# A hybrid decoder block in float32 pairs: norm statistics from rows of x, and an opening that runs two whole GLU tiles on unnormalised x

## The chip, the cores and the metric

The kernel runs on one core of a Trainium2 chip. The metric is the time of the whole program in device microseconds, the median of three runs. The engines are TensorE (PE, matmuls), VectorE (DVE), ScalarE (ACT), GpSimd (POOL) and SyncE (SP), which issues all the transfers here.

## The reference, cut to what matters

One decoder layer over 2048 positions of width 1024. An RMS norm is followed by one wide projection into GLU halves, a convolution gate, queries, keys, values, an attention gate and merge gates. A depthwise convolution branch (31 taps, layer norm, SiLU) and a windowed attention branch are gated, projected, merged and projected again, with a residual and a final RMS norm.

```
def rmsnorm(x, g):
    y = x * lax.rsqrt(jnp.mean(x * x, axis=-1, keepdims=True) + RMS_EPS)
    return y * g

h = rmsnorm(x, norm_g)
proj = h @ w_in      # glu a, glu b, conv gate, q, k, v, attention gate, merge gates
c = silu(layernorm(depthwise_conv(a * sigmoid(b)), ln_g, ln_b))
y_conv = (c * silu(conv_gate)) @ w_conv_out
y_attn = (attention(rope(q), rope(k), v) * silu(attn_gate)) @ w_attn_out
x = x + (g_conv * y_conv + g_attn * y_attn) @ w_out
return rmsnorm(x, final_norm_g)
```

The statistic of the norm is one number per position: the mean of 1024 squares. A projection of normalised x is the projection of `x * g` times that position's `1 / rms`.

## The kernel before, in words

The positions are taken in two sweeps (`NSWEEP`) of 1024, and each sweep in two halves of `TH` = 512. Within a sweep x is held transposed: eight tiles `k` of 128 channels by 512 positions per half. Each float32 operand is split into a rounded part `hi` and the rest `lo` (`split_lo`, L233), and one `product` (L269) is three matmuls of 128x128 by 128x512. An output tile of 128 channels takes eight products per half. In the rows, `whi` and `wlo` are the parts of a weight, `hT` those of the normalised x, `u` those of `x * g` without the norm. `mm_` and a name is the PSUM tile of an item: `gb` and `ga` for the GLU, `ka`, `kb`, `q_a`, `q_b`, `v`, then the gates, `ya`, `yc`, and `o` for the last projection.

TensorE's instructions run in the order in which the program writes them. The other engines' orders and SP's queue are chosen at compile time by a list scheduler, by priority and readiness; program order gives the priority, and `tc.high_priority` raises it. At run time every engine takes its instructions in order.

`Line` (L159) is a planner with a clock of its own. It runs items, each a prefetch and a generator of blocks. The prefetch of an item is called ahead of the blocks of the item before it. Each block yields its cost on TensorE (`MM_US` = 0.2275 a matmul). In `spend` (L167) the clock moves on, background operations (`bg`) are taken one per `every` microseconds, and chains that are due are advanced. The convolution is background work: 31 operations on VectorE per channel tile, queued when a GLU tile's second half has left PSUM (`ev_a`, L532), one per 3.2 us (`ROPE_EVERY`) until attention starts and one per 2.4 us (`CONV_EVERY`) from then. When the last of eight tiles is done, `ln_chain` (L801) and `ln_chain2` (L813) put four matmuls each for mean and variance into TensorE's order, and then `ln_recip`, `ln_apply` and `u_op` (L839) follow as background operations, one per 1.6 us. `u_op` loads a stored gate (`lcg`), multiplies and splits. The first `ya` item's eviction (L901) writes `mp`, whose slot the last reader of the convolution's result must have freed; if the first `u_op`s have not been issued by then, it calls `line.finish()`, which issues all the rest ahead of it.

`norm_chain` (L324) takes the sum of squares per position, still spread over 128 partitions, splits it, multiplies it with `ones` (1/1024 in every cell), which sums over partitions and puts the mean into all of them, and takes the root and the reciprocal of 128x512 numbers into `rs`.

`opening` (L354) is the start of sweep 0. `first_blocks` runs `gb`, `ga` and `ka` of half 0 on `u` as the x tiles land, with the squares on ScalarE and their sums on VectorE beside it. Then `kb`, `q_a` and `q_b` of half 0 run on `u`, while the squares of half 1 are summed on POOL; the norm of half 1 stands after three products of the last of them. `both_halves_done` runs `gb` and `ga` of half 1 on `hT`, and the four remaining items run their half 1 on `hT`, while `put_h` (L344) makes the tiles of half 0. What was computed on `u` is multiplied by `rs` when it leaves PSUM (`un`, L396). From then on all items read `hT`. A second GLU tile follows at index 6 of `others`, by `GLU_AFTER`.

In the last projection of sweep 0, `prepare` (L965) gets sweep 1's x ready after each output block: `next_square` loads column tiles (`xs`), squares them on ScalarE and sums on POOL, `next_norm` starts the chain after blocks 4 and 8 (its matmuls come 6 us later on the planner's clock), and `next_h` loads again (`xh`) and makes `hT`.

Of the kernel before, what the change touches and what calls it, by code (L numbers as in the profile page):

```python
# [12 lines left out]
F32 = mybir.dt.float32  # L13
# [40 lines left out]
def hybrid_block(ctx: ExitStack, tc: tile.TileContext, x, xt, par_d, w_in, w_conv, sinks, w_attn, w_out,  # L54
# [181 lines left out]
    def load_w(src, name, home=None, steps=None):  # L236
# [4 lines left out]
        def part(kh):  # L241
# [74 lines left out]
    def add_square(raw, total, k, name, eng):  # L316
        if k == 0:
            act.activation(out=total, in_=raw, func=AF.Square)
        else:
            sq = t2k(name)  # L320
            act.activation(out=sq, in_=raw, func=AF.Square)
            eng.tensor_tensor(out=total, in0=total, in1=sq, op=ALU.add)

    def norm_chain(total, rs, wait, name):  # L324

        hi, lo = (t2k(f"{name}{p}", F32R) for p in "hl")
        act.copy(hi, total)
        split_lo(lo, total, hi, dve)
        yield 0.0, wait
        ms = small_bank(f"{name}ms")  # L330
        for i, part in enumerate((hi, lo)):
            pe.matmul(out=ms, lhsT=ones, rhs=part, start=(i == 0), stop=(i == 1))
        act.activation(out=rs, in_=ms, func=AF.Sqrt, bias=eps)
        for i in range(2):
            c = rs[:, i * (TH // 2):(i + 1) * (TH // 2)]
            dve.reciprocal(out=c, in_=c)
# [17 lines left out]
    def opening(items, load_rope):  # L354


        (pa, pb, pc_), rest = [it[2] for it in items[:3]], [it[2] for it in items[3:]]
        xr = [slot(A[i], [P, 2, TH], F32, f"xr0_{i}") for i in range(4)]
        raw = [[xr[k // 2][:, k % 2] for k in range(KC)], []]
        u = [slot((C[0:7] + A[5:6])[k], [P, 2, TH], F32R, f"u{k}") for k in range(KC)]  # L360
        total = work.tile([P, 2, TH], F32, tag="ln0", name="total0", bufs=1)
        rs = slot(X[0], [P, 2, TH], F32, "rs0")
        homes = [[slot(H[3 * i + j], [P, 2, 4, P], F32R if j else F32, f"w{i}_{j}") for j in range(3)]
                 for i in range(2)]
        ws, steps = [], []
        for i, (src, name, _) in enumerate((pa, pb)):
            steps.append([])
            ws.append(load_w(src, name, homes[i], steps[i]))
        steps.append([])
        ws.append(load_w(pc_[0], f"{pc_[1]}0", None, steps[2]))  # L370
        stats = {}

        def ready(k):
            load_x(0, 0, k, raw[0][k])
# [726 lines left out]
```

## Time and profile before

| What | us |
|---|---|
| median of three runs | 2057.91 (2057.75 to 2058.42) |
| the profiled execution's own time | 2059.32 |
| span of the profile | 2057.4 |
| mean granted TensorE clock | 0.988 of full |

The profile's page gives the busy time of each engine, then the span in 40 slices, the queues, the chain that ended last and the costliest groups of instructions. A group's row has the line, the engine, the operation, the tiles written and read, their shapes, and the count; behind the first bar stand the busy time in us and the mean of one in ns, behind the second the idle time of the engine ahead of it and what ended that. A timeline row has the start and the length in us, then engine, line, operation and tiles. A row of the waits has who waited, for whom, the total in us, how often, and the longest.

### The profile page before, as it was taken

How to read it: one execution, taken by the hardware profiler on the slowest of the kernel's cores; microseconds unless marked ns; L12 is line 12 of the kernel's file. 1: busy time of each engine (PE TensorE's matmuls, PEld its weight loads, DVE VectorE, ACT ScalarE, POOL GpSimd, SP SyncE). 2: the span in 40 equal slices, each digit the busy share in tenths (PEclk: the TensorE clock that was granted, in tenths of full speed). 3: DMA queues.
4: the chain of work that ended last, by engine and by line, in shares of the span. 5: the costliest groups of instructions: out<-in, count | busy, mean ns of one | idle time of the engine just before them, and what ended most of it. 6: DMA issues, size and time to landing. Idle time of an engine off the chain costs nothing.

```text
span 2057.4 us, 27299 instructions
## 1 busy us (share of the span) xinstructions
PE 2001.0 (97%) x9136; PEld 1660.0 (81%) x9136; DVE 1356.2 (66%) x1921; ACT 1025.7 (50%) x2249; POOL 439.1 (21%) x354
## 2 busy tenths in 40 slices
PE   6899999999999996999999999999999999999998
PEld 4688888888888884888788888888888888888887
DVE  7889679989995156123559686699888935341324
ACT  5432377767777354112432324777777774621222
POOL 5234332333233222243301020110111010000200
PEclk9899999999999998999999999999999999999999
DMA  7445555455556755446455356555555568474432
GB/s 253 148 135 174 174 180 164 159 178 179 164 176 206 249 190 193 149 139 231 160 184 165 110 165 215 165 177 170 171 166 167 179 222 261 165 242 148 148 118 82
DMA packets 269852, 361.14 MB, mean 176 GB/s; under 512 B 28560, under 2 KB 126992, under 8 KB 269712
## 3 DMA queue, kind: packets, MB, share of 16 engines
q1 hardware_dynamic: 269712, 359.40, 53.7%
q8 instruction: 72, 1.18, 0.2%
q14 instruction: 68, 0.56, 0.1%
HBM read 239.75 MB, written 119.54 MB: 175 GB/s over the span
## 4 chain that ended last, share of the span: by engine, by line
PE 59%; DVE 1%; DMA 1%; issue 0%; ACT 0%; DVEq 0%; SPq 0%; ACTq 0%
PE mm_yc L271 8%; PE mm_ya L271 8%; PE o L1025 7%; PE mm_ma L271 4%; PE mm_cg L271 4%; PE mm_ag L271 4%; PE mm_gb L271 4%; PE mm_ga L271 4%; PE mm_mc L271 4%; PE mm_q_b L271 2%; PE mm_q_a L271 2%; PE sc L683 1%; PE ov L733 1%; PE mm_v L271 1%; PE tpp L713 1%; PE mm_ka L271 1%
## 5 line engine op out<-in xcount | busy, mean ns | idle before, releaser
L507 DVE SCALAR_TENSOR_TENSOR acc<-glu,par,acc 128x1024 f32<-128x1024 f32 x464 | 596.1, 1285 | 6.2
L271 PE MATMUL mm_ya<-aT,whi_ya 128*128 128x512 f32 x512 | 159.4, 393 | 20.3 <-DVE mp L906 20.3
L1025 PE MATMUL o<-wo,mT 128*128 128x512 f32 x768 | 175.1, 389 | 1.0 <-DVE wo L234 1.0
L1025 PEld LDWEIGHTS o<-wo,mT 128*128 128x128 f32 x768 | 144.1, 188 | 31.3 <-DVE wo L234 1.4
L271 PE MATMUL mm_ma<-hT,whi_ma 128*128 128x512 f32 x512 | 159.7, 393 | 0.0
L271 PE MATMUL mm_cg<-hT,whi_cg 128*128 128x512 f32 x512 | 159.7, 393 | 0.0
L271 PE MATMUL mm_ag<-hT,whi_ag 128*128 128x512 f32 x512 | 159.4, 393 | 0.0
L271 PE MATMUL mm_mc<-hT,whi_mc 128*128 128x512 f32 x512 | 158.0, 390 | 0.0
L271 PE MATMUL mm_yc<-uT,whi_yc 128*128 128x512 f32 x512 | 157.6, 389 | 0.0
L724 POOL TENSOR_SCALAR_AFFINE_SELECT pc<-pt 128x1024 fp32r<-128x1024 f32 x60 | 65.6, 1094 | 422.5 <-DVE pt L234 416.7
L271 PE MATMUL mm_gb<-hT,whi_gb 128*128 128x512 f32 x480 | 149.5, 393 | 0.0
L271 PE MATMUL mm_ga<-hT,whi_ga 128*128 128x512 f32 x480 | 149.1, 392 | 0.0
L271 PEld LDWEIGHTS mm_ya<-aT,whi_ya 128*128 128x128 f32 x512 | 97.1, 190 | 41.0 <-DVE mp L906 20.7
L271 PEld LDWEIGHTS mm_yc<-uT,whi_yc 128*128 128x128 f32 x512 | 96.1, 188 | 19.9
L271 PEld LDWEIGHTS mm_mc<-hT,whi_mc 128*128 128x128 f32 x512 | 96.0, 188 | 20.1
L271 PEld LDWEIGHTS mm_ag<-hT,whi_ag 128*128 128x128 f32 x512 | 94.2, 188 | 18.3
L271 PEld LDWEIGHTS mm_cg<-hT,whi_cg 128*128 128x128 f32 x512 | 94.1, 188 | 18.3
L271 PEld LDWEIGHTS mm_ma<-hT,whi_ma 128*128 128x128 f32 x512 | 94.1, 188 | 18.2
L703 ACT ACTIVATE ss<-ss,st 128x128 f32<-128x128 f32 x256 | 99.7, 391 | 11.2 <-DVE st L698 10.6
L271 PEld LDWEIGHTS mm_ga<-hT,whi_ga 128*128 128x128 f32 x480 | 88.8, 188 | 17.6
L271 PEld LDWEIGHTS mm_gb<-hT,whi_gb 128*128 128x128 f32 x480 | 88.5, 188 | 17.5
L271 PE MATMUL mm_ya<-aT,wlo_ya 128*128 128x512 f32 x256 | 100.3, 392 | 0.0
(436 smaller groups left out, 4319.2 us busy)
## 6 DMA issues: line engine op xcount, KB each, us to landing
qk<-d_q SPq DMA_DIRECT2D x256, 64.0 KB, 2.2
d_a<-ss SPq DMA_DIRECT2D x128, 128.0 KB, 1.9
aT<-d_a SPq DMA_DIRECT2D x32, 512.0 KB, 5.5
qk<-d_k SPq DMA_DIRECT2D x240, 64.0 KB, 2.0
raw_ag<-in_w_in_dram SPq DMA_DIRECT2D x32, 256.0 KB, 3.8
d_ag<-ag SPq DMA_DIRECT2D x32, 256.0 KB, 2.2
ss<-d_ag SPq DMA_DIRECT2D x64, 128.0 KB, 2.6
raw_cg<-in_w_in_dram SPq DMA_DIRECT2D x32, 256.0 KB, 3.4
```

The lines of the kernel that those rows point to most:

```text
L271: pe.matmul(out=ps, lhsT=a, rhs=b, start=(k == 0 and i == 0), stop=(k == KC - 1 and i == 2))
L507: dve.scalar_tensor_tensor(out=to, in0=glu[c][:, j:j + T], scalar=tap(c, j), in1=acc[c], op0=ALU.mult, op1=ALU.add)
L683: pe.matmul(out=o, lhsT=q[:, h, :], rhs=r, start=(j == 0), stop=(j == 1))
L703: act.activation(out=sb[:, h, :], in_=sb[:, h, :], func=AF.Exp, scale=SCALE, bias=ngm[:, h:h + 1], accum_out=den[:, h:h + 1])
L713: pe.transpose(out=tpp[:, h, :], in_=sb[:, h, :], identity=ident)
L724: pool.affine_select(out=pc, in_=f(pt), pattern=[[0, 2], [0, GQ], [1, P]], compare_op=ALU.is_ge, fill=0.0, base=0, channel_multiplier=-1)
L733: pe.matmul(out=ov, lhsT=vv, rhs=pp[:, i % 2], start=(i == 0), stop=(i == nm - 1))
L1025: pe.matmul(out=ps, lhsT=a[:, c0:c0 + P], rhs=r, start=(k == 0 and i == 0), stop=(k == KC - 1 and i == 2))
```

## The change

Five things change.

1. The sum of squares comes from rows. A tile of 128 positions by 1024 channels of x is loaded, and one ScalarE instruction squares it and sums along the row (`row_square`), which gives one number per partition; four such tiles make a half. The root and the reciprocal are taken of 128x4 numbers. A diagonal matrix of 128x512 with these numbers (`dg`) is split, and the matmul with `ones` spreads each number to all partitions; a copy scaled by 1024 writes `rs`. The wide root and reciprocals and the sums on VectorE and POOL are gone.
2. The opening runs both halves of two GLU tiles (four items) on `u` and no key or query item. It loads, in this order: x of half 0 with the first two weights between, x of half 1, two row tiles of half 0, the third and the fourth row tile of half 0, each followed by one of the other two weights, the four row tiles of half 1, the sinks. The norm of half 0 stands in TensorE's order after 35 products, that of half 1 after 51 of the 64.
3. `hT` of half 0 is made after the fourth item's first half and `hT` of half 1 after the third item's second half; the first reader of either is `ka`, behind the opening.
4. In both sweeps the two value items come ahead of the query items, and the second GLU tile is no longer at index 6.
5. For sweep 1, `next_square` loads half rows (128 positions by 512 channels) instead of column tiles, and `next_norm` starts after blocks 3 and 7.

Also, in the opening both weight steps of an item are split on VectorE instead of the first one only.

```diff
-                split_lo(lo, raw, hi, dve if steps is not None and kh == 0 else pool)
+                split_lo(lo, raw, hi, dve if steps is not None else pool)
...
-    def add_square(raw, total, k, name, eng):
-        if k == 0:
-            act.activation(out=total, in_=raw, func=AF.Square)
-        else:
-            sq = t2k(name)
-            act.activation(out=sq, in_=raw, func=AF.Square)
-            eng.tensor_tensor(out=total, in0=total, in1=sq, op=ALU.add)
+    def row_square(x, out_, ss):
+        act.activation(out=out_, in_=x, func=AF.Square, accum_out=ss)
+
+    def norm_chain(ss, bank, rs, wait, name):
+        rt = work.tile([P, 2, 4], F32, tag="rt", name=f"{name}rt")
+        act.activation(out=rt[:, 0], in_=ss, func=AF.Sqrt, bias=eps, scale=1.0 / D)
+        dve.reciprocal(out=rt[:, 1], in_=rt[:, 0])
+        dg = t2k(f"{name}d").rearrange("p (b t) -> p b t", t=P)
+        dve.tensor_tensor(out=dg, in0=ident.unsqueeze(1).broadcast_to([P, 4, P]),
+                          in1=rt[:, 1].unsqueeze(2).broadcast_to([P, 4, P]), op=ALU.mult)
+        dg = dg.rearrange("p b t -> p (b t)")
         hi, lo = (t2k(f"{name}{p}", F32R) for p in "hl")
-        act.copy(hi, total)
-        split_lo(lo, total, hi, dve)
+        act.copy(hi, dg)
+        split_lo(lo, dg, hi, dve)
         yield 0.0, wait
-        ms = small_bank(f"{name}ms")
+        ms = bank()
         for i, part in enumerate((hi, lo)):
             pe.matmul(out=ms, lhsT=ones, rhs=part, start=(i == 0), stop=(i == 1))
-        act.activation(out=rs, in_=ms, func=AF.Sqrt, bias=eps)
-        for i in range(2):
-            c = rs[:, i * (TH // 2):(i + 1) * (TH // 2)]
-            dve.reciprocal(out=c, in_=c)
+        act.activation(out=rs, in_=ms, func=AF.Copy, scale=float(D))
...
+        def prefetch2():
+            for k in range(KC):
+                load_x(0, 1, k, raw[1][k])
+            for half in range(2):
+                for j in range(4):
+                    r0 = (4 * half + j) * P
+                    nc.sync.dma_start(out=rows[half][j], in_=x2[r0:r0 + P, :])
+                    if half == 0 and j > 1:
+                        for kh in range(2):
+                            steps[j][kh]()
+            load_sinks()
...
+            for half in range(2):
...
+                for k in range(KC):
+                    scaled_split(u[half][k], raw[half][k], k)
+                    for i in range(2):
+                        product(ps[i, half], ws[i][0](k), u[half][k], k)
                         yield 3 * MM_US
+            squares(0)
...
+                    if i == 2 and k == 2:
+                        yield spread(half)
+                        if half == 0:
+                            squares(1)
...
+                if half == 0 and i == 3:
+                    ht[0] = make_tiles(h_tags[0], 0, "hT0_")
+                    for k in range(KC):
+                        put_h(ht[0][k], raw[0][k], rs[:, 0], k)
+                if half == 1 and i == 2:
+                    ht[1] = make_tiles(h_tags[0], 1, "hT0_")
+                    for k in range(KC):
+                        put_h(ht[1][k], raw[1][k], rs[:, 1], k)
...
+        yield prefetch, first_blocks
+        yield prefetch2, later(2, 0)
+        yield (lambda: None), later(3, 0)
+        yield (lambda: None), later(2, 1)
+        yield (lambda: None), later(3, 1)
...
-        others = rope_items("k", E_K, store_k)
+        others = rope_items("k", E_K, store_k) + [v_item(i) for i in range(2)]
...
-            yield from opening(glu_items(0) + others[:4], load_rope)
-            glu_after.pop(0)
+            yield from opening(glu_items(0) + glu_items(1))
+            glu_after = glu_after[2:]
...
+        def next_square(b):
+            if b % 4 == 0:
+                nx["ss"] = work.tile([P, 3, 4], F32, tag="ss", name=f"ss{s + 1}_{b}")
+            r0 = (s + 1) * T + b * P
+            for i in range(2):
+                raw = raw_tile(f"xs{s + 1}_{b}_{i}")
+                nc.sync.dma_start(out=raw, in_=x2[r0:r0 + P, i * TH:(i + 1) * TH])
+                row_square(raw, t2k(f"sq{s + 1}_{b}_{i}"), nx["ss"][:, i, b % 4:b % 4 + 1])
...
-            if i in (4, 8):
-                line.start(next_norm(i // 4 - 1))
+            if i in (3, 7):
+                line.start(next_norm(i // 4))
```

`spread(half)` runs `norm_chain` at high priority and then `leave` for the first two items: multiply by `rs`, then the item's own eviction. `later(i, half)` runs one half of the third or fourth item.

More of the change, by code (lines that the diff above doesn't have):

```diff
@@ L352, in hybrid_block, with opening @@
     ht = [None, None]
[L354 to L361, printed above, removed]
+    def opening(items):
+        parts = [it[2] for it in items]
+        names = [A[0:4], A[14:16] + X[1:3]]
+        raw = []
+        for half in range(2):
+            pair = [slot(t, [P, 2, TH], F32, f"xr{half}_{t}") for t in names[half]]
+            raw.append([pair[k // 2][:, k % 2] for k in range(KC)])
+        u = [[slot(t, [P, 2, TH], F32R, f"u{half}_{t}") for t in tags]
+             for half, tags in enumerate((C[0:6] + A[4:6], A[6:11] + A[13:14] + H[14:16]))]
+        rows = [[slot(t, [P, D], F32, f"row_{t}") for t in tags]
+                for tags in (H[8:12], H[12:14] + H[6:8])]
@@ L362, in opening @@
         rs = slot(X[0], [P, 2, TH], F32, "rs0")
[L363 to L364 removed]
+        ss = work.tile([P, 2, 4], F32, tag="ss0", name="ss0", bufs=1)
+        acc = cv_ps.tile([P, T], F32, tag="acc", name="rs_bc")
         ws, steps = [], []
[L366 removed]
+        for i, (src, name, _) in enumerate(parts):
+            home = [slot(H[3 * i + j], [P, 2, 4, P], F32R if j else F32, f"w{i}_{j}")
+                    for j in range(3)] if i < 2 else None
@@ new lines, in leave, with squares @@
+        def leave(i, half, ps):
+            with tc.high_priority(offset=PRIO):
+                t = t2k(f"un{i}_{half}")
+                dve.tensor_tensor(out=t, in0=ps, in1=rs[:, half], op=ALU.mult)
+                parts[i][2](half, t)
+        ps = {}
+        def squares(half):
+            for j in range(4):
+                row_square(rows[half][j], rows[half][j], ss[:, half, j:j + 1])
+        def first_blocks():
+            for half in range(2):
+                for i in range(2):
+                    name = f"mm_{parts[i][1]}0{half}"
+                    ps[i, half] = (small_bank(name) if half and i else
+                                   mm_ps.tile([P, TH], F32, tag="mm", name=name))
+                for k in range(KC):
+                    scaled_split(u[half][k], raw[half][k], k)
+                    for i in range(2):
+                        product(ps[i, half], ws[i][0](k), u[half][k], k)
@@ L408, in first_blocks, with spread @@
                         yield 3 * MM_US
-            for k in range(2):
-                ws[2][1](k)
+            squares(0)
+        def spread(half):
+            chain = norm_chain(ss[:, half], lambda: acc[:, half * TH:(half + 1) * TH], rs[:, half], 0.0, f"n{half}")
             with tc.high_priority(offset=2 * PRIO):
-                steps_ = list(norm_chain(total[:, 0], rs[:, 0], 0.0, "n0"))
-            yield sum(us for us, _ in steps_)
-            with tc.high_priority(offset=PRIO):
-                for p, b in zip((pa, pb, pc_), ps):
-                    after_rs(p[2])(0, b)
@@ L463, in opening @@
-        yield (lambda: None), both_halves_done
-        def put_some(ks):
-            if ks[0] == 0:
-                ht[0] = make_tiles(h_tags[0], 0, "hT0_")
-            for k in ks:
-                put_h(ht[0][k], raw[0][k], rs[:, 0], k)
-        for i, (src, name, evac) in enumerate([pc_] + rest):
-            pre, blocks, _ = project(src, lambda k, half: ht[1][k], f"{name}1", evac, (1,))
-            def with_h(blocks=blocks, i=i):
-                put_some((2 * i, 2 * i + 1))
-                yield from blocks()
-            yield pre, with_h
+                us = sum(c[0] for c in chain)
```

118 lines of the change are left out of this document (35 added, 83 removed).

## The prediction

> **What bounds the kernel now.** I read the page's engine table first, then the list of what TensorE waited for, then the busy time by stretches of the span, then single rows of the timeline around the two places that these views point to.
>
> ```profile
> span 2057.4 us, 27299 instructions
> ...
> PE 2001.0 (97%) x9136; PEld 1660.0 (81%) x9136; DVE 1356.2 (66%) x1921; ACT 1025.7 (50%) x2249; POOL 439.1 (21%) x354
> ```
>
> TensorE is busy for 97% of the span, so the change can win only what TensorE loses in gaps and at a low clock, unless it alters the matmuls. It doesn't: the opening has 96 `product` calls of three matmuls and four matmuls with `ones` for the same outputs, before and after.
>
> ```profile
> PE mm_ya L271 <- DVE mp L906: 20.3, 1, 20.3
> PE n1ms L332 <- ACT n1h L327: 12.9, 1, 12.9
> PE mm_gb L271 <- ACT w L249: 7.9, 1, 7.9
> PE mm_gb L271 <- ACT hT L340: 4.2, 2, 2.8
> PE mm_gb L271 <- DVE hT L341: 1.9, 2, 1.6
> ```
>
> Columns: total, times, longest. Nearly all idle time stands here. Four of the five rows lie in the opening. The first is at the seam of sweep 0, where the first `ya` tile cannot leave PSUM.
>
> ```profile
> 0.00:14.40 14.40, 6.51 (x18) 4.44 (x19) 8.37 (x18) 9.80 (x17) 2.06 (x9) 1.00 0.84 293
> 14.40:40.40 26.00, 26.00 (x115) 21.20 (x113) 22.45 (x21) 15.01 (x26) 17.17 (x12) 1.00 0.78 259
> 40.40:53.30 12.90, 0.02 (x1) 0.00 (x0) 10.84 (x11) 3.42 (x7) 10.12 (x7) 0.62 0.61 214
> 62.20:75.00 12.80, 9.46 (x22) 6.43 (x23) 12.52 (x18) 5.14 (x8) 3.90 (x3) 0.60 0.45 144
> 787.00:807.00 20.00, 0.00 (x0) 0.00 (x0) 12.84 (x22) 6.53 (x11) 5.71 (x2) 0.60 0.54 186
> ...
> 102.81 0.39 PE L271 MATMUL mm_v<-hT,whi_v 128*128 128x512 f32 x1
> ...
> 1067.65 10.88 PE mm_ga L271 x48
> ```
>
> A stretch lists PE, PEld, DVE, ACT and POOL busy (with counts), then the granted clock, DMA share and GB/s. The last row is from the chain: 48 matmuls in 10.88 us, 0.2267 each at full clock, 0.68 a product. The opening's 292 matmuls are worth 66.2 us and `mm_v`, the first item behind them, starts at 102.81: the opening loses 36.6 us. Of that 10.3 fall before 14.4 (18 matmuls, 4.1 us of work), 12.9 in the wait for `n1h`, 6.1 in the waits for `hT`, and the other 7.3 are half clock: 0.60 granted from 62.2 to 75.
>
> **The start.** Squares and sums leave ScalarE's and VectorE's queues; the two first weights' splits go wholly to VectorE. A `k` has now two products, 1.36 us, against one x tile and half a weight step on ScalarE (0.72 + 0.3) and VectorE (0.74 + 0.35), by these rows:
>
> ```profile
> L340 ACT ACTIVATE hT<-xr,par 128x512 fp32r<-128x512 f32 x8 | 5.5, 718 | 4.8 <-PE mm_gb L271 4.6 <-DVE xr L345 0.3
> L249 ACT CAST w<-w 128x512 fp32r<-128x512 f32 x4 | 2.4, 602 | 0.0
> L345 DVE TENSOR_TENSOR xr_x<-xr_x,rs 128x512 f32<-128x512 f32 x4 | 2.6, 682 | 0.0
> L341 DVE SCALAR_TENSOR_TENSOR hT<-xr_x,par,hT 128x512 fp32r<-128x512 f32 x4 | 2.8, 744 | 0.0
> 8.00:12.00 4.00, 3.99 (x9) 2.38 (x10) 4.00 (x8) 4.00 (x8) 0.00 (x0) 1.00 1.04 374
> ```
>
> So TensorE sets the pace after the first landing; I keep the 10.3 us of loss. Second-half x tiles are queued right behind the first: 5.4 MB with `par` and weights. The queue moved 293 GB/s up to 14.4 us (4.2 MB) and 374 at its best, so they are in by 17.6, and the second half's first product comes at 10.3 + 16 x 0.68 = 21.2. No wait.
>
> **Row statistics, half 0.** The rows cost 4 MB more for the opening, half of it and 0.5 MB of weight ahead of the first norm's last row tile. That is 8.0 MB: 14.4 + 3.8/0.374 = 24.6 us. No 1024-wide square with a sum is in the trace; the rows below bound it at 1.25 + 0.18 us, so the last ends at about 26.5. Then root, small reciprocal, diagonal, `hi`, `lo`: about 0.3 + 0.2 + 0.69 + 0.62 + 0.69, ready near 29. TensorE gets to this matmul after 35 products, at 34.1. Five us of slack hide all of it; with the DMA 5 us later it would cost what exceeds that. The wait that is added is TensorE's on the diagonal: behind it in its order stands everything else, and behind a square that waits for its row on ScalarE stand the casts of the later weights and `rs` itself. Half 1's rows end near 31.6, its matmul stands after 51 products at 45.5, and 5.7 us of squares, a table load of 1.28 and the chain fit between. The 12.9 us wait, its POOL sums and the four wide reciprocals (6.7 us of VectorE) go. On SP's queue the 4 MB push the rope tables, the sinks and `ka`'s weights back by 11 us, to about 32; the first of them is wanted at 54.7, so this costs nothing unless the queue stands still for 20 us.
>
> ```profile
> 785.58 1.25 ACT L799 ACTIVATE cv<-cv,par 128x1024 f32<-128x1024 f32 x1 [0.52 <-DVE cv L798]
> 995.72 0.18 ACT L995 ACTIVATION_READ_ACCUMULATOR ysq<-y 128x1 f32 x1
> 52.66 0.62 ACT L327 CAST n1h<-total 128x512 fp32r<-128x512 f32 x1 [2.59 <-POOL total L322]
> 53.30 1.28 ACT L333 ACT_TABLE_LOAD   x1
> 53.31 0.69 DVE L234 TENSOR_TENSOR n1l<-total,n1h 128x512 fp32r<-128x512 f32 x1
> 54.89 0.69 ACT L333 ACTIVATE rs<-n1ms,eps_t 128x512 f32<-128x512 f32 x1 [0.31 <-PE n1ms L332]
> L336 DVE RECIPROCAL rs<-rs 128x256 f32<-128x256 f32 x4 | 6.7, 1721 | 2.8 <-ACT rs L333 2.8
> ```
>
> **What is late next: `hT`.** All four GLU items now run on `u`, so `ka` is the first reader of `hT`, at 10.3 + 64 x 0.68 + 0.9 = 54.7, and its half 1 needs the last tile at 64.9. VectorE makes all sixteen, after `rs`: 34.6 + 0.8 = 35.4 for half 0. From there, at 0.68 or 0.69 for an `un` (row below) or a `glu` product: 7 `un` and 3 `glu` 6.9, `put_h` 16 x (0.68 + 0.74) = 22.7, the second norm 1.5, two convolution taps 2.6: 33.7 us, the last `hT` at 69.1. If the taps fall behind it, 66.5. With the last `un` and `glu` (1.4), `ka`'s two rope products (1.4) and four POOL weight splits, each of which lengthens a VectorE instruction from 0.74 to 1.75, 76. I take 72: TensorE waits 7 us (bounds 2 and 11), a little before each product.
>
> ```profile
> 43.33 0.68 DVE L396 TENSOR_TENSOR un<-mm_q_a,rs 128x512 f32<-128x512 f32 x1
> 62.55 1.75 DVE L341 SCALAR_TENSOR_TENSOR hT<-xr_a,par,hT 128x512 fp32r<-128x512 f32 x1
> 86.20 1.28 DVE L507 SCALAR_TENSOR_TENSOR acc<-glu,par,acc 128x1024 f32<-128x1024 f32 x1
> L234 POOL TENSOR_TENSOR wlo_kb<-raw_kb,whi_kb 128x512 fp32r<-128x512 f32 x2 | 3.2, 1636 | 0.2 <-ACT whi_kb L249 0.2
> ```
>
> The Trainium skill ("SBUF — State Buffer", Who interferes with whom) makes this an exclusive lock: two-input VectorE instructions and POOL reads shut each other out for a whole instruction. By it a late VectorE instruction would pay up to POOL's 1.64, and the sum would be some 2.5 us worse; the 1.75 of this trace, 1.0 of delay, is what I use.
>
> For the clock I add 2 us (0 to 4): while VectorE gives a product every 1.42 us, a half-clock product of 1.36 costs nothing, only the return to full clock does. In the stretch from 62.2, gaps of 1 to 3 us came with 0.60. The Trainium skill ("TensorE: Matmul & The Clock Gate", HAM oscillation) halves the clock only after gaps above about 3.4 us; by it this term is nothing and the time 2 us lower. The row of 62.2 is the nearest, so I keep the 2.
>
> The opening then loses 10.3 + 7 + 2 = 19.3 instead of 36.6: 17.3 us gained, bounds 11 to 24.
>
> **The seam of sweep 0.** The planner's clock starts the convolution after 51 products instead of 64, at 35.7 instead of 45.3. At 3.2 us a tap that is three taps more by the start of attention; each remaining one costs 2.4. Counted through with the constants, the variance matmuls come at 716.5 instead of 723.4, while the first `ya` stays at 731.8. `line.finish()` at its eviction then flushes 15 operations instead of 19.
>
> ```profile
> 763.24 1.75 DVE L795 RECIPROCAL rstd<-rstd 128x256 f32<-128x256 f32 x1 [14.15 <-ACT rstd L819]
> 778.92 0.68 DVE L830 TENSOR_TENSOR lcg<-lcg,cv 128x512 f32<-128x512 f32 x1
> 791.52 0.32 SPq L265 DMA_DIRECT2D d_lo<-wlo_ya  x1
> 797.06 0.69 DVE L830 TENSOR_TENSOR lcg<-lcg,cv 128x512 f32<-128x512 f32 x1 [6.69 <-DMA lcg<-d_cg]
> 806.34 0.69 DVE L906 TENSOR_TENSOR mp<-mm_ya,lma 128x512 f32<-128x512 f32 x1 [0.30 <-DMA lma<-d_ma]
> ```
>
> From 763.24 to 806.34 VectorE works through reciprocals, `apply` and `u_op`, except for the 6.7 us in which SP's queue held the `lcg` loads behind the store of `wlo_ya`. Starting 6.9 earlier shortens the 20.3 by up to 6.9; that store keeps to TensorE's position and may take some back. I take 5 (0 to 8).
>
> **The seam between the sweeps.** Second-half statistics are asked for one output block (5.4 us) earlier.
>
> ```profile
> 1008.93 0.33 SPq L314 DMA_DIRECT2D xs<-in_xt_dram  x1
> 1018.03 0.62 ACT L321 ACTIVATE sq<-xs 128x512 f32<-128x512 f32 x1
> 1023.88 0.40 PE L332 MATMUL n11ms<-n11h,ones 128*128 128x512 f32 x1
> ```
>
> TensorE would reach this matmul at 1018.4. Square and sum (0.8 each, two) and a chain of 2.5 leave it ready between 1017, if ScalarE takes the tiles as they land, and 1022, if it keeps to 1018. POOL's adds are gone, and the row loads are as many and as large as the column loads were. I take 1.5 us of loss (0 to 4). The key and value items that change places read the same `hT`: nothing, since TensorE's queue behind them is full.
>
> **The sum.** The profiled execution took 2059.3 around its span of 2057.4, 1.4 above the median of 2057.9. 2059.3 - 17.3 - 5 + 1.5 = 2038.5; against the median 2037.
>
> **The rivals.** A: `hT` comes later still, or the first norm's matmul waits for its rows (in-order ScalarE behind a late tile). Against it stand the 5 us of slack; for it the full DMA queue. It loses up to 10 more: 2044 to 2053, chance 0.2. B: `hT` keeps up, as VectorE puts it ahead of everything, and the seam gives its 6.9: loss 12, 2025 to 2029, chance 0.13. C: no change, since VectorE's rate hands the same 36 us to TensorE in another place: 2058, chance 0.05. It needs the last `hT` at about 93. D, slower: VectorE is contended throughout. Each two-input instruction of `put_h` beside a POOL one costs 1.0 more; break-even lies at about 21 such of 32, all 32 give 11 us more than before, 2069. For it: VectorE is over 90% busy from 62 to 75; against it: POOL has four splits and no sums in that time. Chance 0.08. My forecast, 2030 to 2044, has 0.54.
>
> The 8 in 10 take in the forecast, most of B and of A: 2026 to 2050. Below 0.2% (4 us) a change can't be told from none. Faster 0.87, same 0.05, slower 0.08.
>
> **What would show it.** Right: no wait before the two norm matmuls of the opening; `mm_gb` starting near 7.5 and TensorE gapless to about 55; a row of waits of `mm_ka` for `hT` of 2 to 11 us; the first `mm_v` at 82 to 92 for 292 matmuls less `q0` (it now follows `kb`); the `mp` wait at 12 to 20. Wrong: a wait of `n0ms`, an `mm_ka` wait above 15, or a new wait at the sweeps' seam above 4.

## The result, and the profile after

The changed kernel takes 2036.28 us (median of four runs, 2036.05 to 2036.56). The kernel before took 2058.05 beside it. The ratio is 0.9894, with a 95% interval of 0.9877 to 0.9911. The profiled execution of the changed kernel took 2036.56 with a span of 2034.8 and a mean granted clock of 0.994 (0.988 before).

The forecast of 2037 is met within 1 us, but not by its own sum: three of its terms were off by 3.3 to 5.7 us, and the errors nearly cancelled. The table sets the same piece of work of both traces side by side. "Gained so far" is the difference of the two start times, so a row's own contribution is its difference to the row above.

| First matmul of | before | after | gained so far | this stretch | predicted |
|---|---|---|---|---|---|
| `mm_v`, behind the opening | 102.81 | 81.24 | 21.6 | 21.6 | 17.3 |
| `mm_ya`, ahead of the seam of sweep 0 | 770.3 | 748.9 | 21.4 | -0.2 | 0 |
| `mm_yc`, behind that seam | 880.0 | 850.3 | 29.7 | 8.3 | 5 |
| `mm_gb` of sweep 1, behind the sweeps' seam | 1056.61 | 1034.12 | 22.5 | -7.2 | -1.5 |
| end of the span | 2057.4 | 2034.8 | 22.6 | 0.1 | 0 |

The opening of the changed kernel stands unaltered in three of the kernels below. In their profiles the first `mm_v` comes at 79.55 to 80.82, so a stretch of this table is good to some 1.7 us.

The page of the profile after, its engine table:

```profile
PE 1999.4 (98%) x9136; PEld 1658.5 (82%) x9136; DVE 1337.9 (66%) x1931; ACT 1031.3 (51%) x2271; POOL 395.9 (19%) x328
```

The 9136 matmuls stayed. TensorE's busy time fell by 1.6 us, so most of the 22.6 came out of gaps. What TensorE waited for (total, times, longest):

```profile
PE mm_ya L271 <- DVE mp L888: 12.5, 1, 12.5
PE mm_gb L271 <- ACT w L249: 6.9, 1, 6.9
PE n11ms L334 <- ACT n11h L329: 3.9, 1, 3.9
...
PE mm_ka L271 <- DVE hT L340: 1.2, 2, 0.6
PE mm_ka L271 <- ACT hT L339: 1.1, 2, 0.6
PE n11ms L334 <- DVE n11l L234: 0.7, 1, 0.7
PE rs_bc L334 <- DVE n1l L234: 0.4, 1, 0.4
PE rs_bc L334 <- ACT n1h L329: 0.3, 1, 0.3
```

The 12.9 us at the opening's second norm have become 0.7, the 6.1 us of waits for `hT` 2.3, and the wait for `mp` 12.5 instead of 20.3. The third row is new: it belongs to the norm of sweep 1's second half, in the seam between the sweeps. The opening by stretches (PE, PEld, DVE, ACT and POOL busy, then granted clock, DMA share, GB/s), and single rows of it:

```profile
40.00:55.00 15.00, 14.29 (x62) 11.28 (x61) 14.94 (x23) 11.53 (x18) 4.91 (x4) 1.00 0.37 131
62.00:75.00 13.00, 10.69 (x43) 7.46 (x42) 12.93 (x19) 4.00 (x7) 4.32 (x3) 1.00 0.25 78
```

```profile
26.32 0.18 ACT L317 ACTIVATION_READ_ACCUMULATOR row_h<-row_h 128x1 f32 x1
29.74 0.69 DVE L234 TENSOR_TENSOR n0l<-n0d,n0h 128x512 fp32r<-128x512 f32 x1 [0.69 <-ACT n0h L329]
33.81 0.39 PE L334 MATMUL rs_bc<-n0h,ones 128*128 128x512 f32 x1
55.78 0.62 PE L271 MATMUL mm_ka<-hT,whi_ka 128*128 128x512 f32 x2
68.93 0.73 DVE L340 SCALAR_TENSOR_TENSOR hT<-xr_x,par,hT 128x512 fp32r<-128x512 f32 x1
...
70.31 0.63 PE L271 MATMUL mm_kb<-hT,whi_kb 128*128 128x512 f32 x2
81.24 0.61 PE L271 MATMUL mm_v<-hT,whi_v 128*128 128x512 f32 x2
```

Read them against the forecast. The norm of half 0 is ready at 30.43 and wanted at 33.81. `ka` starts at 55.78. From there to `kb` pass 14.53 us for 16 products that are worth 10.88, so the late `hT` costs 3.65. The clock is 1.00 in every stretch from 14.4 to 75.

### The profile page after: what moved, and what is told of

Same layout as the page of the kernel before. It is cut to its first block, busy times and chain, and to the rows that moved or that the text cites. A ratio compares the mean times of both kernels' runs of the same rounds, so it can differ in the third digit from the quotient of the medians.

```text
span 2034.8 us, 27254 instructions
## 1 busy us (share of the span) xinstructions
PE 1999.4 (98%) x9136; PEld 1658.5 (82%) x9136; DVE 1337.9 (66%) x1931; ACT 1031.3 (51%) x2271; POOL 395.9 (19%) x328
## 4 chain that ended last, share of the span: by engine, by line
PE 51%; DVE 1%; DMA 0%; issue 0%; ACT 0%; DVEq 0%; ACTq 0%
PE o L1012 6%; PE mm_ma L271 4%; PE mm_cg L271 4%; PE mm_ag L271 4%; PE mm_gb L271 4%; PE mm_ga L271 4%; PE mm_mc L271 4%; PE mm_yc L271 4%; PE mm_ya L271 4%; PE mm_q_a L271 2%; PE mm_q_b L271 2%; PE sc L668 2%; PE ov L718 1%; PE mm_v L271 1%; PE tpp L698 1%; PE mm_kb L271 1%
## 5 line engine op out<-in xcount | busy, mean ns | idle before, releaser
L271 PE MATMUL mm_ya<-aT,whi_ya 128*128 128x512 f32 x512 | 158.9, 392 | 12.5 <-DVE mp L888 12.5
L271 PE MATMUL mm_gb<-hT,whi_gb 128*128 128x512 f32 x448 | 139.2, 392 | 0.0
L271 PE MATMUL mm_ga<-hT,whi_ga 128*128 128x512 f32 x448 | 139.2, 392 | 0.0
L271 PEld LDWEIGHTS mm_ya<-aT,whi_ya 128*128 128x128 f32 x512 | 96.8, 189 | 33.0 <-DVE mp L888 12.9
L688 ACT ACTIVATE ss<-ss,st 128x128 f32<-128x128 f32 x256 | 99.7, 390 | 11.3 <-DVE st L683 10.7
L271 PE MATMUL mm_ma<-hT,wlo_ma 128*128 128x512 f32 x256 | 99.9, 390 | 0.0
L271 PE MATMUL mm_cg<-hT,wlo_cg 128*128 128x512 f32 x256 | 99.9, 390 | 0.0
```

Source lines behind the costliest of these rows:

```text
L271: pe.matmul(out=ps, lhsT=a, rhs=b, start=(k == 0 and i == 0), stop=(k == KC - 1 and i == 2))
L688: act.activation(out=sb[:, h, :], in_=sb[:, h, :], func=AF.Exp, scale=SCALE, bias=ngm[:, h:h + 1], accum_out=den[:, h:h + 1])
```

## The experiments

The theory after these readings names three places, each with its own cause. In the opening the order of the work pays (nothing but `u` is needed for 64 products), and the rows make the chains short enough to keep up. At the seam of sweep 0 it is the planner's clock, which starts the convolution earlier. At the sweeps' seam the norm is asked for one block too early. The rivals: the rows alone, or the order alone, do it all; the seam's gain comes from SP's queue; the new wait comes from the rows' loads.

**Late norms.** The changed kernel, with the two norms between the sweeps started one block later, ahead of that block's own work:

```diff
+            if i in (4, 8):
+                line.start(next_norm(i // 4 - 1))
             if i < 8:
                 next_square(i)
-            if i in (3, 7):
-                line.start(next_norm(i // 4))
```

> The changed kernel with sweep 1's two norms asked for ahead of the squares of block 4 and of block 8, as before the change; the squares still come from rows. Theory (the earlier place is what costs): in the changed kernel the first output block of sweep 1 starts 22.5 us earlier than before while the last projection of sweep 0 starts 29.7 us earlier, so 7.2 us are lost there, 4.6 of them in the waits for n11h and n11l and the rest at half clock behind them. With the matmul 5.4 us later on TensorE the chain, ready near 993, is done in time: the waits of n11ms go to under 0.5 and the time falls by about 7, to 2029. Rival (row statistics themselves are too slow there, by ScalarE's 16 sums and the row loads behind the w_out loads): the chain moves later with its place, the wait stays near 4 us and the time near 2036.

It took 2029.94 us (2028.82 to 2030.65), ratio to before 0.9866 [0.9851, 0.9880]. The seam's stretches and rows in the changed kernel, first, and here:

```profile
988.40:994.40 6.00, 1.38 (x3) 0.97 (x4) 5.74 (x12) 4.00 (x10) 0.00 (x0) 0.87 0.92 326
994.40:1002.00 7.60, 7.60 (x24) 5.95 (x24) 5.34 (x9) 1.91 (x4) 0.00 (x0) 0.66 0.49 158
```

```profile
986.57 0.63 ACT L982 ACTIVATE ysq<-y 128x512 f32<-128x512 f32 x1 [1.90 <-DVE y L981]
...
987.20 0.61 ACT L317 ACTIVATE sq<-xs 128x512 f32<-128x512 f32 x1
...
988.42 1.32 ACT L339 ACTIVATE hT<-xh,par 128x512 fp32r<-128x512 f32 x2
989.65 0.28 ACT L322 ACTIVATE n11rt<-ss,eps_t 128x4 f32<-128x4 f32 x1
...
991.63 0.62 ACT L329 CAST n11h<-n11d 128x512 fp32r<-128x512 f32 x1 [0.47 <-DVE n11d L325]
...
992.30 0.50 PE L334 MATMUL n11ms<-n11h,ones 128*128 128x512 f32 x1 [3.93 <-ACT n11h L329]
993.52 0.79 PE L334 MATMUL n11ms<-n11l,ones 128*128 128x512 f32 x1 [0.72 <-DVE n11l L234]
```

```profile
988.40:994.40 6.00, 5.18 (x24) 3.96 (x23) 6.00 (x13) 3.65 (x8) 0.00 (x0) 1.00 0.85 321
994.40:1002.00 7.60, 7.60 (x35) 6.27 (x34) 7.07 (x13) 3.77 (x9) 0.00 (x0) 1.00 0.63 233
```

```profile
991.63 0.62 ACT L329 CAST n11h<-n11d 128x512 fp32r<-128x512 f32 x1
...
992.85 0.39 PE L334 MATMUL n11ms<-n11h,ones 128*128 128x512 f32 x1
994.06 0.50 PE L334 MATMUL n11ms<-n11l,ones 128*128 128x512 f32 x1 [0.82 <-DVE n11l L234]
```

The chain's `hi` is ready at the same moment in both, 991.63 + 0.62, and its `lo` half a us later here. What has moved is the place of its matmul in TensorE's order, and that is worth all of it: 59 matmuls pass from 988.4 to 1002 instead of 27, 32 x 0.2267 = 7.25 us. By the medians 6.3 us were won where 7 were expected, and a wait of 0.8 us is left. Behind the wait of 3.93 us the granted clock was 0.66 over 7.6 us; behind the wait of 0.82 here it was 1.00.

Two things made the chain late. The squares that open it, at 987.20 in the changed kernel, stood in ScalarE's order behind `ysq`, which waited for VectorE, which was splitting `wo`. And the chain took twice its own work: from the end of the squares at 988.52 to the end of `lo` at 993.47 pass 4.95 us, where the forecast had counted 2.5, since `hT` tiles of the other half stood between its steps on ScalarE and on VectorE. It wasn't the row loads: the last one was issued at 979.61.

**The second norm alone.** The same, for the second half's norm only:

```diff
-            if i in (3, 7):
-                line.start(next_norm(i // 4))
+            if i in (3, 8):
+                line.start(next_norm((i - 3) // 5))
```

> The changed kernel with only the second norm of sweep 1 moved back (asked for after block 8); the first stays after block 3. Theory (only the second norm's place costs, since the first one's matmul waited 0.25 us): same gain as with both moved, 2029. Rival (an early first norm makes its h tiles' loads sit in the staging buffers and so delays the last row tiles): it gains less than half of it, 2033 or more.

The median is 2036.12, as without the edit, but one of the four runs took 2029.62. The profiled one (2036.52) has no wait for `n11h` any more, and from the first `o` to sweep 1's first `mm_gb` pass 88.9 us, as with both norms moved (89.1), instead of 96.8. So this edit mends the seam too. The rival's figure came, but not its mechanism. What the edit won was lost elsewhere: TensorE waits 4.4 us ahead of `mm_mc`, and the first `mm_ya` starts at 754.9 instead of 748.9. Two views of that execution:

```profile
703.15 11.89 POOL L234 TENSOR_TENSOR wlo_mc<-raw_mc,whi_mc 128x512 fp32r<-128x512 f32 x1 [8.83 <-ACT whi_mc L249]
```

```profile
L234 POOL TENSOR_TENSOR wlo_mc<-raw_mc,whi_mc x16: 1282/1289/11895, 640.7 to 733.9; 128x512 fp32r<-128x512 f32 x16
```

The last row is a group's: shortest, median and longest in ns. One GpSimd split out of 16 took 11.89 us instead of 1.29. SP's queue issued nothing from 701.9 to 715.07, where it waited to store that split's result. VectorE ran two-input operations without a pause from 701.51 to 713.9 beside it. In the changed kernel's profile the same split begins at 703.23, in the same run of VectorE operations, and takes 1.40. There VectorE gave way instead. Its operations at that moment, here and then in the changed kernel:

```profile
703.31 2.35 DVE L766 TENSOR_TENSOR cv<-cv,mu 128x1024 f32<-128x1024 f32 x2
```

```profile
703.39 4.56 DVE L766 TENSOR_TENSOR cv<-cv,mu 128x1024 f32<-128x1024 f32 x2
```

**That split on VectorE.** To test this, the kernel just told of, with the splits of `mc`'s weights moved off GpSimd:

```diff
-                split_lo(lo, raw, hi, dve if steps is not None else pool)
+                split_lo(lo, raw, hi, dve if steps is not None or name.startswith("mc") else pool)
```

> The kernel with only its second late norm mended (median 2036.1, one of four runs 2029.6) lost in its profiled run 4.4 us of waiting, and half clock behind it, near 720 us: a GpSimd split of a weight of mc, 1.29 us as a rule, took 11.89 us from 703.15 while VectorE ran two-input operations back to back from 701.5 to 713.9. Here all 16 splits of mc's weights run on VectorE instead, nothing else is changed. Theory (GpSimd gets no turn while VectorE's two-input operations follow one another): no wait of mm_mc over 1 us, all runs within 2028 to 2031.5. Rival (the late start comes from the queue of DMAs or from ScalarE): the wait stays, most runs at 2035 to 2037. Second rival (the splits now wait in VectorE's own queue behind the 10 us of variance): a wait of mm_mc of 2 us or more in all runs, 2032 to 2038.

All four runs lie between 2028.41 and 2030.33, median 2029.50, ratio 0.9864 [0.9848, 0.9881]. There is no wait of `mm_mc`. The long GpSimd split was the cause in the profiled run; the two other runs near 2036 have no trace.

**The convolution's start put back.** The changed kernel, with the planner's clock for the convolution held back by the 9.6 us that the new opening wins for it:

```diff
                         if half == 0:
                             squares(1)
                         if half:
+                            line.bg_t = line.t + 9.6
```

> The changed kernel with the convolution's first background operation held back by 9.6 us on the planner's clock, so that it starts at 45.3 as before. Theory (the seam of sweep 0 gained because the planner takes three taps more before attention, which brings the variance matmuls 6.9 us nearer to the start and shortens the flush from 19 operations to 15): the wait of mm_ya for mp returns from 12.5 to about 20 and the time rises by 7 to 8, to 2044. Rival (the seam gained since the order of the queue at the seam changed: no 6.7 us stall of the lcg loads behind the store of wlo_ya): the wait stays at 12 to 14 and the time at 2036 to 2038.

2040.64 (2038.52 to 2041.58), ratio 0.9917 [0.9902, 0.9931]. The wait for `mp`, and the rows at both ends of VectorE's work ahead of it, here and then in the changed kernel:

```profile
PE mm_ya L271 <- DVE mp L889: 17.9, 1, 17.9
```

```profile
741.79 6.59 DVE L781 RECIPROCAL rstd<-rstd 128x256 f32<-128x256 f32 x4 [14.74 <-ACT rstd L805]
782.86 0.69 DVE L889 TENSOR_TENSOR mp<-mm_ya,lma 128x512 f32<-128x512 f32 x1
```

```profile
736.02 6.59 DVE L780 RECIPROCAL rstd<-rstd 128x256 f32<-128x256 f32 x4 [15.24 <-ACT rstd L804]
...
777.17 0.69 DVE L888 TENSOR_TENSOR mp<-mm_ya,lma 128x512 f32<-128x512 f32 x1
```

Counted from the first `ya`, the reciprocals start 7.5 us ahead here, 12.9 in the changed kernel and 7.1 in the kernel before. From there to `mp` it is 41.1, 41.2 and 43.1. So 5.4 of the 7.8 us by which this wait shrank are the planner's clock. Some 2 us are a shorter way to `mp`. Of the stall of 6.69 us for `lcg` on SP's queue at most 2.61 is left in one and 0.80 in the other. In the changed kernel most of that went again: four `uT` operations of VectorE took 1.74 to 1.78 us there instead of 0.68, beside GpSimd's splits of `wlo_ya`, 4.3 us in all. Two of the four stand in this row:

```profile
758.02 4.09 DVE L234 TENSOR_TENSOR uT<-lcg,uT 128x512 fp32r<-128x512 f32 x3
```

**The convolution earlier still.**

```diff
-ROPE_EVERY = 3.2
+ROPE_EVERY = 3.0
```

> The changed kernel with one convolution tap per 3.0 us of the planner's clock ahead of attention instead of 3.2. By the constants the variance matmuls then come at 709.7, and three u operations stand ahead of the first ya eviction, so that the flush is not called. Theory (the flush ahead of the first eviction is what TensorE waits for): the 12.5 us wait goes to 2 or less and the half clock behind it goes too, 2036 - 15 = 2021. Rival (VectorE's own work between the variance and the first eviction is the bound, whatever the planner calls): the wait falls only by the 6.8 us that the variance moves, to about 5.5, and the time to 2028 to 2030. A second rival: VectorE, over 90% busy in the opening's hand-over, takes the denser taps there and hT comes later, up to 3 us worse.

2022.71 (2022.18 to 2023.09), ratio 0.9831 [0.9814, 0.9847]: 13.6 us under the changed kernel. The wait for `mp` is gone altogether; now VectorE waits for TensorE there:

```profile
729.92 6.59 DVE L780 RECIPROCAL rstd<-rstd 128x256 f32<-128x256 f32 x4 [14.02 <-ACT rstd L804]
...
748.86 2.92 DVE L815 TENSOR_TENSOR lcg<-lcg,cv 128x512 f32<-128x512 f32 x3 [2.05 <-DMA lcg<-d_cg]
755.25 0.69 DVE L888 TENSOR_TENSOR mp<-mm_ya,lma 128x512 f32<-128x512 f32 x1 [3.47 <-PE mm_ya L271]
```

The reciprocals came 6 us earlier than in the changed kernel, but `mp` 22. By the planner's constants the first `u_op`s are now issued ahead of that eviction, so that `line.finish()` no longer puts all the rest in front of `mp`. The trace agrees: three `lcg` products stand ahead of the first `mp` in VectorE's order, and sixteen in the changed kernel. This term has a step in it.

**The order with columns.** The changed kernel's order in the opening, with column sums (half 0 on VectorE, half 1 on GpSimd) and the wide root and reciprocals; the core of the edit:

```diff
+                    add_square(raw[half][k], total[:, half], k, f"sq{half}_{k}", pool if half else dve)
...
-            chain = norm_chain(ss[:, half], lambda: acc[:, half * TH:(half + 1) * TH], rs[:, half], 0.0, f"n{half}")
+            chain = col_chain(total[:, half], lambda: acc[:, half * TH:(half + 1) * TH], rs[:, half], 0.0, f"n{half}")
```

> The changed kernel with its order of the opening kept (both halves of the two GLU tiles on raw x, tiles copied out at once, the row of the sinks loaded in the opening), but the statistics of the opening taken from columns again: ScalarE squares the blocks, VectorE adds half 0, GpSimd half 1, and the wide root and reciprocals make rs (6.7 us of VectorE reciprocals per half in the trace of before). The two seams stay as in the changed kernel. Theory (the order is what pays in the opening; rows are worth the shorter chains and the idle VectorE): the wait at the norm of half 0 stays under 1 us because its matmuls have 14 us of other work ahead, but 14 sums of 0.7 us and 13 us of reciprocals lie before the last hT, so the hand-over waits 4 to 10 us longer than the 3.7 us of the changed kernel: first mm_v at 85 to 92 instead of 81.2, median 2040 to 2048. Rival (the rows are what pays, the order alone gives little): the norm of half 1 waits as in before, first mm_v near 98 to 103, 2053 to 2058. Second rival (the statistics are hidden either way): first mm_v within 1 us of 81.2, 2036.

2048.86 (2047.70 to 2050.22), ratio 0.9962 [0.9948, 0.9976]. The first `mm_v` is at 94.5, worse than the theory had it, because of a wait that nobody had named:

```profile
18.85 5.86 DVE L363 SCALAR_TENSOR_TENSOR u_a<-xr_a,par,u_a 128x512 fp32r<-128x512 f32 x4
...
19.27 11.62 POOL L344 TENSOR_TENSOR total<-total,sq 128x512 f32<-128x512 f32 x7 [17.14 <-ACT sq L343]
...
32.84 1.22 PE L271 MATMUL mm_gb<-u_a,w 128*128 128x512 f32 x2 [4.70 <-DVE u_a L363]
```

Four VectorE operations of 0.75 us took 5.86 beside GpSimd's sums. The 6.7 us of reciprocals that the expectation counts for each half are those of both halves, 3.4 for each.

**The order with columns, all sums on VectorE.** One argument of the last kernel:

```diff
-                    add_square(raw[half][k], total[:, half], k, f"sq{half}_{k}", pool if half else dve)
+                    add_square(raw[half][k], total[:, half], k, f"sq{half}_{k}", dve)
```

> The run before last with column statistics in the opening's new order (2048.9 us) had a wait of 4.7 us for a block u at 32.84 us that the changed kernel doesn't have: seven GpSimd sums took 11.62 us between 19.27 and 30.9, and four VectorE operations of 0.75 took 5.86 us there. Here those seven sums run on VectorE (0.69 us each, 4.8 us more on its queue), and GpSimd has nothing to do in that stretch. Theory (the two engines held each other up): the wait for u falls under 1.5 us and its half clock goes, first mm_v 88 to 91 instead of 94.5, median 2042.5 to 2046; what is left against the changed kernel's 81.2 is the price of columns, through the 3.4 us pairs of reciprocals and the longer chain. Rival (the u blocks come late from VectorE's sheer number of operations): the wait stays at 3.5 us or more, 2047.5 to 2051.

Two runs took 2042.7 and 2043.1, two 2047.9 and 2048.9 (ratio 0.9941 [0.9924, 0.9959]); the first kind was profiled. The two others lie in the rival's range, have no trace, and what they lose is not known. In the profile the wait for `u` is 0.18 and the first `mm_v` comes at 88.5. In this trace seven more operations on VectorE were cheaper than the same seven on GpSimd beside it, as the theory had it. The last 7.3 us against the changed kernel's 81.24 are the price of columns: the waits of `ka` for `hT` are 6.7 in all instead of 2.3, and they cost clock.

```profile
PE mm_ka L271 <- ACT hT L362: 3.7, 3, 2.8
PE mm_ka L271 <- DVE hT L363: 3.0, 4, 1.3
```

```profile
59.00:61.00 2.00, 0.67 (x2) 0.19 (x1) 2.00 (x3) 1.00 (x2) 0.00 (x0) 1.00 0.77 253
61.00:63.00 2.00, 1.58 (x5) 0.82 (x5) 2.00 (x4) 0.00 (x0) 0.00 (x0) 0.83 0.04 8
63.00:65.60 2.60, 0.00 (x0) 0.00 (x0) 2.60 (x5) 0.76 (x2) 1.26 (x1) 0.50 0.00 0
```

**Rows in the old order.** The kernel before with row statistics in its opening only; its seams and the order of its matmuls stay:

```diff
+            for j in range(4):
+                load_row(0, j)
...
-                add_square(raw[0][k], total[:, 0], k, f"sq0_{k}", dve)
...
+            squares(0)
...
-                steps_ = list(norm_chain(total[:, 0], rs[:, 0], 0.0, "n0"))
+                steps_ = list(row_chain(ss[:, 0], rs[:, 0], "n0"))
```

> The kernel before with one part of the change: the opening's statistics from rows with the diagonal matrix, rows of half 0 loaded behind x of half 0, rows of half 1 among the later loads; the order of the matmuls of before stays (half 0 of three tiles, then the rest), and so do both seams (columns). Theory (the order pays): the wait of 12.9 us at the second norm falls to at most 4, with part of the half clock behind it; the waits for hT stay; first mm_v at 88 to 96 instead of 102.8, median 2043 to 2051. Rival (rows alone do all of it): first mm_v under 84, 2039 or less. Rival (eight more row loads on SP delay the weights as much as the shorter chain gains): first mm_v within 3 us of 102.8, 2055 to 2061.

2051.05 (2049.64 to 2054.19), ratio 0.9977 [0.9966, 0.9987]; first `mm_v` at 97.0 in the profiled execution (2053.35), 5.8 us earlier than before.

```profile
PE n1ms L354 <- ACT n1h L349: 6.6, 1, 6.6
PE mm_q_b L271 <- ACT whi_q_b L249: 5.0, 1, 5.0
```

```profile
39.92 1.57 SPq L625 DMA_DIRECT2D d_k<-hl_k  x2
41.55 0.49 SPq L248 DMA_DIRECT2D raw_q_b<-in_w_in_dram  x1
```

Both waits have one cause, and half of the third rival is in it: SP's queue issued nothing from 27.6 to 39.92, where it waited to store the first keys, and the row loads had pushed a weight of `q_b` and the last rows (issued at 42.09) behind that store. So rows alone give 5.8 us, the order alone (with the sums on VectorE) 14.3, and both together 21.6. Neither does it alone. In the new order no key is stored ahead of the rows, and the last of them is issued by 23.7.

**Two parts costed at nothing.** First the changed kernel with the second weight steps split by GpSimd again:

```diff
-                split_lo(lo, raw, hi, dve if steps is not None else pool)
+                split_lo(lo, raw, hi, dve if steps is not None and kh == 0 else pool)
```

> The changed kernel with its first hunk undone: the second halves of the opening's weight pieces are split by GpSimd again, not by VectorE. Theory (nothing waits for these splits while TensorE works on the first tiles): first matmul and first mm_v within 1 us of the changed kernel, 2035 to 2038. Rival (GpSimd's 1.3 us split and its contention with VectorE make the first matmuls or the last hT late): a wait of 1 to 4 us appears in the first 20 us or at mm_ka, 2037.5 to 2041.

2036.62 (2036.05 to 2042.49), ratio 0.9909 [0.9894, 0.9924]: no difference to the changed kernel in the median. One wait of `mm_ka` for `hT` is 1.8 us long, as the rival had it, but the first `mm_v` comes at 80.5. One of the four runs is 6 us longer than the others, for no known reason. Then the value items behind the first query pair again:

```diff
-        others = rope_items("k", E_K, store_k) + [v_item(i) for i in range(2)]
+        others = rope_items("k", E_K, store_k)
         for r in range(GQ):
             others += rope_items(f"q{r}_", E_Q + 2 * r, store_q(r))
+            if r == 0:
+                others += [v_item(i) for i in range(2)]
```

> The changed kernel with its fourth part undone: in both sweeps the two value items stand behind the first query pair again, instead of ahead of it. Theory (as the prediction costed it, nothing: all of them read the same hT and TensorE's queue behind them is full): 2035.5 to 2037.5, the start of attention and of the first mm_ag within 1 us of the changed kernel. Rival (the value items ahead of the query pair give VectorE, which is 90% busy and hands over hT until 70 us, a stretch of TensorE work with little for VectorE; with the rope products of q0 there instead, something waits): a new wait of 2 us or more before 120 us, 2038 to 2042.

2035.96 (2034.99 to 2036.62), ratio 0.9888 [0.9872, 0.9905]: nothing either, and no wait that the changed kernel doesn't have but 0.2 us of `lnvar`.

**Both repairs.** The late norms and `ROPE_EVERY` 3.0 together, the two edits shown above:

> The changed kernel with both repairs that the first runs pointed to: the two norms of the seam between the sweeps are asked for ahead of the squares of blocks 4 and 8 (minus 6 to 7 us alone), and ROPE_EVERY 3.0 lets the planner run the convolution earlier, so that its variance is ready before the mixing (minus 13.6 us alone). Theory (the two lie in different places and add up): no wait of mm_ya for mp, no wait of n11ms over 1 us, 2014.5 to 2017. Rival (the earlier convolution moves work into the place that the late norms need, or the other way round): a new wait of 3 us or more, 2018 to 2023.

2016.82 (2015.62 to 2017.21), ratio 0.9805 [0.9791, 0.9820]. They add up: 6.3 + 13.6 are 19.9, and 19.5 came. And the same with `mc`'s splits on VectorE, the third edit shown above:

> The kernel with both repairs of the seams (late norms, earlier convolution; 2016.8 median), with the splits of mc's weights on VectorE as in the kernel where that took away the long GpSimd split. Theory (its variance is still computed by two-input VectorE operations back to back beside those splits, so a GpSimd split is held for up to 6.9 us there, but nothing waits for it): 2015.5 to 2017.5, no change beyond 1 us. Rival (part of the time is lost to it): the small waits of mm_mc (0.9 us) go, 2014 to 2015.5. Second rival (16 splits more on VectorE delay the variance, which must be ready for the first ya): a wait of mm_ya for mp comes back, 2018 to 2024.

2015.22 (2014.50 to 2015.99), ratio 0.9788 [0.9773, 0.9802]. The two intervals overlap, so the last step is not told apart from nothing. The longest of the splits in the kernel without this edit took 5.2 us; the expectation's 6.9 is a row of two. TensorE is now busy for 99% of the span.

## Why the prediction was right, and where it was not

**The start and the norms.** The sum kept 10.3 us of loss and nothing for the norms, with `ka` at 54.7. It is 55.78, 11.3 us behind the 196 matmuls ahead of it. The start itself lost 10.0: the norm of half 0, behind 105 matmuls, is at 33.81. TensorE's first matmul was 1 us earlier (6.9 instead of 7.9), but that gave little: in both traces the products up to 12 or 13 us start 1.1 to 1.7 us apart, busy and not waiting, and 0.68 apart only from then on. Why they are slow isn't shown; the profile gives the clock as 1.00 there. The other 1.3 us went at the second norm. Its two matmuls took from 45.19 to 46.90, with two waits of 0.7 in all, since `hT` tiles stood ahead of its diagonal's two parts in ScalarE's and VectorE's queues. The forecast had named no wait there. The rows were in when they were forecast: the last square of half 0 ended at 26.50 (26.5), the chain at 30.43 (29), since a square of half 1 and a cast of a weight stood between its steps on ScalarE. The slack was 3.4 us instead of 5 and hid everything. A square with its sum took 1.06 + 0.18, below the bound of 1.25 + 0.18.

**The hand-over of `hT`: the mechanism right, the size wrong.** `ka` is the place, VectorE the cause, and a short wait ahead of each product the form. But the last `hT` ended at 69.66, not 72. The chosen value stood between 69.1 and 76, and the upper part was made of the last `un`, `glu` and rope products, 2.8 us, and of four GpSimd splits that each lengthen a VectorE operation by 1.0. Those products did come ahead of the last `hT`. Of the `hT` operations three were lengthened, by 1.8 us in all. The rows of one group (shortest, median and longest in ns), and one run of another:

```profile
L340 DVE SCALAR_TENSOR_TENSOR hT<-xr_a,par,hT x12: 736/743/1475, 40.0 to 62.7; 128x512 fp32r<-128x512 f32 x12
```

```profile
63.33 1.88 DVE L344 TENSOR_TENSOR xr_x<-xr_x,rs 128x512 f32<-128x512 f32 x3
```

The second row is what made the sum too large. It added each operation at its full recorded length, but here three of 0.68 took 1.88, since each starts some 0.08 before the row of the last one ends. From 35.09 to 69.66 VectorE's rows add up to 38.4 us in a stretch of 34.6. So a wait of 7 came out as 2.3 (bounds 2 and 11), and the whole loss is 3.65. The first `mm_v`, at 81.24, lies 0.8 ahead of the 82 to 92 that the forecast named.

**The clock term fell.** The 2 us came from the stretch at 62.2 of the trace before, where gaps of 1 to 3 us went with a clock of 0.60. The gaps are now 0.55 to 0.61 us, and 62 to 75 shows 1.00. That row was the nearest in time and place but not in the length of its gaps. The other branch, by which this term is nothing, held; where the limit lies, gaps this short do not show. With `hT` and clock together 3.65 instead of 9, the opening gave 21.6 instead of 17.3, within its bounds of 11 to 24.

**The seam of sweep 0: right, and too small.** The planner's clock is shown as the cause by the run that puts it back. Its 5.4 us are less than the 6.9 that were counted through. The store of `wlo_ya` did not take some back. The stall behind it shrank instead, and the way to `mp` with it by 2 us, which no run tests by itself. The stretch gave 8.3 instead of 5, just beyond its bounds of 0 to 8.

**The seam between the sweeps: the step that failed.** The text put the chain's readiness between 1017 and 1022 on the time axis of before, and took 1.5 us of loss (0 to 4). On that axis (29.7 us later) it was ready at 1022.0 with `hi` and 1023.2 with `lo`, at and beyond the late end. "If ScalarE takes the tiles as they land" was the branch that should have been given up: in ScalarE's order `ysq`, which waits for VectorE, stood in front of these squares. They began at 1016.9 on that axis, 1.1 us ahead of the late branch's 1018. What carried the chain past 1022 is its own length, 4.95 us instead of 2.5, which the sum took as if nothing stood between its steps. And the term had no clock: the wait of 3.93 us is followed by 7.6 us at 0.66. Both together are 7.2 us, and this is the one loss that the change brought. Among the signs of a wrong forecast "a new wait at the sweeps' seam above 4" came true with 3.9 + 0.7.

**The rivals.** A (rows or `hT` later) and D (VectorE contended throughout) did not come. B's came in good part: `hT` nearly kept up (a loss of 15.0 in the opening; B had 12, the forecast 19.3), and the seam gave more than its 6.9. B gave 2025 to 2029, and the kernel with the late norms takes 2029.9. So the middle of the forecast was met only because the failed step took back what the other two gave. That is luck.

## What to carry to other kernels

Before a chain of statistics is asked for earlier, list what stands in front of its first instruction on its in-order engine, and put its matmul in TensorE's order where the chain is ready, not where its data are. An opening gains when the first stretch of matmuls needs only raw data, but statistics then have to be short for the consumer behind it; here the order alone won 14.3 us, the short chain alone 5.8, and both together 21.6. When a sum comes out right, set it against the trace place by place: a term that failed by 5.7 us was worth a repair of 6.3, and a planner's constant beside the change was worth 13.6.

## What the runs showed of the hardware

A GpSimd operation can be kept out for a whole run of VectorE operations: 11.89 us instead of 1.29, beside 12 us of two-input operations back to back, ending 1.15 us behind the last of them. With nearly the same start against the same run it took 1.40 in the changed kernel, and VectorE's two operations 4.56 instead of 2.35. In the kernel with columns GpSimd's seven sums took 11.62 and four VectorE operations 5.86 instead of 3.0, so there the two seem to have taken turns. The Trainium skill ("SBUF — State Buffer", Who interferes with whom) lets whoever issues first hold the shared ports for one instruction, and has the issue order decide who blocks. The traces agree that either engine can be the one that waits; the 11.89 us are many instructions long and not one. What decides is not shown here.

The granted clock fell after less idle time than expected. In the kernel with columns and VectorE sums it fell to 0.83 on average already from 61 to 63, after waits of 0.27 and 1.27 us since 59, and ahead of the 2.83 us wait that begins at 62.8; from 63 it was 0.50. In the changed kernel, four waits of 0.55 to 0.61 us in 64 to 70 left it at 1.00. The Trainium skill ("TensorE: Matmul & The Clock Gate", HAM oscillation) names idle gaps of more than about 3.4 us; the first case speaks against that limit, and the second agrees with it. How much idle time in how long a stretch decides is not settled by these runs.
